# Three stages of a hybrid decoder step begin with another order of their seven products, and the entries of the feed-forward start are cast, split and summed in another order

## The chip, the cores and the metric

The kernel runs on one core of one Trainium2 chip. The metric is the device time of one launch in microseconds, the median of three runs. The core has a matrix engine (TensorE, PE in the profile), a vector engine (VectorE, DVE), an activation engine (ScalarE, ACT), a general engine (GpSimd, POOL) and a synchronising engine (SyncE, SP), which here only issues DMAs. Each engine executes its own queue in order and waits on semaphores of the others. Matmuls accumulate in banks of PSUM; DVE and ACT read those banks and write SBUF.

## The reference

One layer of a decoder on 512 prompt tokens and 8 sample tokens, with a model width of 2048 and a feed-forward width of 5632, in float32. What matters here, cut from the reference (the mixers' inside, the caches and the states are left out):

```python
def modulate(h, shift, scale):
    return h * (1.0 + scale) + shift

def conv_ffn(h, conv_state, w_ffn_in, conv_w, conv_b, w_ffn_out):
    T = h.shape[1]
    a, g = jnp.split(h @ w_ffn_in, 2, axis=-1)
    ap = jnp.concatenate([conv_state.astype(a.dtype), a], axis=1)
    ac = sum(conv_w[j] * ap[:, j:j + T] for j in range(CONV_W)) + conv_b
    out = (jax.nn.gelu(ac) * g) @ w_ffn_out
    return out, ap[:, ap.shape[1] - (CONV_W - 1):]
```

Ahead of this the normalised input is multiplied by `w_in`, which gives the mixers' inputs and the sigmoid gates of their outputs; the two mixers' outputs are projected, gated and added, and the sum is multiplied by `w_out` and added to the residual stream. The result, normalised and modulated, is the `h` of `conv_ffn`.

## The kernel before

The 520 tokens are two halves of 260 columns (`HN`), the 2048 channels 16 chunks of 128. For each multiplication of float32 precision both operands are split into a high part (a cast, on ACT, named `wh`, `hi` or the first half of `bf`, `mf`, `hf`) and a low part (the difference, on DVE, `wl`, `lo`), and each term is three matmuls: high by high, high by low, low by high (`three_of`).

The large stages multiply two blocks of weights by two halves of the channels and two halves of the tokens with seven products instead of eight. `Pair` (lines 256 to 338) is one such unit: seven products of 8 x 3 = 24 matmuls of 128 x 260, numbered 1 to 7. Products 1, 6, 7 and 4 accumulate one after another in the bank `x`, 5 and 3 in `y`, 2 in `z`. Product 1 takes the weights as they are, and so do 2 and 4; 5, 6, 3 and 7 take sums of weights, the totals 1, 2, 4 and 3 (`sw`), which `total` makes on DVE. `split` makes a product's `wh` and `wl`. Between two products of one bank `take` copies the bank to SBUF (`tt` after product 1 and after the first one in `y`, `tg` after 6) on ACT, and the next product into that bank waits for the copy; the combinations (`c12`, `c22`, `c11`) work on the copies. The order of the products in a unit is one of two tuples:

```python
ORDER, ORDER1 = (1, 5, 6, 3, 7, 2, 4), (1, 2, 3, 5, 6, 7, 4)
```

In `ORDER` the banks are x, y, x, y, x, z, x, in `ORDER1` x, z, y, y, x, x, x. The first unit of three stages has `ORDER1`, all others have `ORDER`. `run_pairs` goes through the products of all units, step by step, `7 * len(units)` of them: at step t it does what is due after the product before (`take`), prepares a product one or two steps ahead (`ahead`: splits and totals; `early` is 1 or 2), then any work listed for that step in the dictionary `late`, and at last issues the product. From `T, V, S = (Ordered(...))` on, the instructions of PE, DVE and ACT stay in the order in which they are written (line 60 is that helper, so they all carry L60); ahead of it a scheduler decides.

The three stages:

- The gates (from 554 us): `units` of `GatePair` and `ValuePair`. The first unit follows the projection of the stage before.
- w_out (from 1330 us): `units` of `WoPair`, which multiply the gated mixers' output `mg` (tiles `sgm`). In the loop over `w_pb` ahead of it each of 16 accumulations `pb` is multiplied by its gate and added to `mgo` (lines 1646, 1647). `m_first` and `m_forms` then make the seven forms of the tokens that the products use, from sums and differences of the chunks i and 8 + i; the forms 6 and 4 (`mf`) of the chunks below 7 are stored to DRAM (`dxf`) and loaded again later, so that their tiles are free meanwhile. The last chunk, 7, is made at the end of the loop.
- The feed-forward (from 1497 us). The first three feature chunks f are multiplied without the seven products, since their tokens' forms come one by one: `features(e, z)` makes the high and low parts of `h` for half e of the channels and half z of the tokens; `beside` and `eight(u, o, e, zs, w)` multiply an entry, which is the weight block (chunk u, o = 0 for the convolved and 1 for the gate side, half e) as it is, by them: 48 matmuls for both halves of the tokens. `sums_of(i)` turns the tokens of the chunks i and 8 + i into the sums that the seven products need, four operations on DVE each using the result of the one before; `sum_parts(n)` makes their high and low parts for product n. `parts2` makes an entry's `wh` and `wl`; `whole_conv(f)` and `whole_gate(f)` end a chunk (copy, convolution, Gelu, gate). Then come the units of `FfnPair`, from f = 3 on, the first of which begins at 1573.8 us.

Of the kernel before, what the change touches and what calls it, by code (L numbers as in the profile page):

```python
# [63 lines left out]
def tile_hybrid_step(ctx: ExitStack, tc: tile.TileContext, I, O):  # L64
# [189 lines left out]
    ORDER, ORDER1 = (1, 5, 6, 3, 7, 2, 4), (1, 2, 3, 5, 6, 7, 4)  # L254

    class Pair:
# [3 lines left out]
        def __init__(self, rows, X, order, early):  # L260
            self.rows, self.X, self.order, self.early = rows, X, order, early
            self.w, self.s = {}, {}
            self.uses = {(0, 0): 3, (1, 0): 2, (0, 1): 2, (1, 1): 2, 1: 2, 2: 2, 3: 1, 4: 1}
# [13 lines left out]
        def total(self, n):  # L277

            a, b = {1: ((1, 0), (1, 1)), 2: (1, (0, 0)), 4: ((0, 1), 2), 3: ((0, 0), (1, 0))}[n]
# [34 lines left out]
        def take(self, n):  # L314

            steady = self.order == ORDER
            if n == 1:
                self.tt = self.temp("tt")
                S.copy(self.tt[:, :HN], self.x)
            if n == (5 if steady else 3):  # L320
                S.copy(self.tt[:, HN:N], self.y)
            if n == 5 and not steady:
                V.tensor_tensor(self.tt[:, HN:N], self.y, self.tt[:, HN:N], op=ALU.subtract)
            if n == 6:
                self.tg = self.temp("tg")
                S.copy(self.tg[:, :HN], self.x)
            if n == (3 if steady else 6):
                self.c12()
            if n == 7:
                self.c22()  # L330
            if n == (2 if steady else 7):
                self.c11()
# [709 lines left out]
    class GatePair(Pair):  # L1042
        def __init__(self, gates, order):
            self.gates = gates
            super().__init__([I["w_in"][49 + g] for g in gates], hX, order, 1)
# [77 lines left out]
    units = [GatePair(gates[2 * i:2 * i + 2], ORDER if i else ORDER1) for i in range(len(gates) // 2)]  # L1123
# [361 lines left out]

    def m_forms(i):

        a, b = mg[i], mg[8 + i]
        mX[2][i], mX[3][i] = hl_parts(hp, "hl", b)
        b11, b12, b21, b22 = (t[:, o:o + HN] for t in (a, b) for o in (0, HN))  # L1490
        V.tensor_tensor(b11, b11, b12, op=ALU.subtract)
        V.tensor_tensor(b12, b22, b12, op=ALU.subtract)
        V.scalar_tensor_tensor(b22, b22, -1.0, b11, op0=ALU.mult, op1=ALU.subtract)
        V.scalar_tensor_tensor(b21, b22, -1.0, b21, op0=ALU.mult, op1=ALU.subtract)
        mX[5][i], mX[7][i] = hl_parts(hp, "hl", a)
        for n, f in ((6, b22), (4, b21)):
            t = (st if i == 7 else pt)("mf", F32R)
            hi, lo = mX[n][i] = parts_of(t)
            S.copy(hi, f)
            V.tensor_tensor(lo, f, hi.bitcast(F32), op=ALU.subtract)  # L1500
            if i < 7:
                G.dma_start(dxf[i + 8 * (n == 4)][:, :N], t[:, :N])
        mg[i] = mg[8 + i] = None
# [110 lines left out]
    for n, j in enumerate(order):  # L1614
# [31 lines left out]
        V.tensor_tensor(z2(mg[j]), acc, z2(mg[j]), op=ALU.mult)  # L1646
        V.tensor_tensor(mg[j][:, :N], mg[j][:, :N], old[:, :N], op=ALU.add)
        if j < 8:
            m_first(j)
        else:  # L1650
            m_forms(j - 8)
# [21 lines left out]
    def parts2(u, o, e):  # L1673
        return wtwo([raws.pop((u, o, e))], 1024)

# [33 lines left out]
    def first_weights(o):  # L1709
# [5 lines left out]
        9: log_exp, 50: lambda: fetch_xa(range(8)), 51: lambda: (load2(0, 0, 0), load2(0, 1, 0)), 53: tot_parts,  # L1715
# [79 lines left out]
    def whole_conv(f):  # L1795
        at = new_at()
        for z in range(2):
            S.copy(at[:, 2 + z * HN:2 + (z + 1) * HN], acc[f][0][z])
        acc[f][0] = None
        part[f] = conv_start(f, at)  # L1800
# [11 lines left out]
    def sums_of(i):  # L1812

        a, b = xa[i], xa[8 + i]
        b11, b12, b21, b22 = a[:, :HN], a[:, HN:N], b[:, :HN], b[:, HN:N]
        V.tensor_tensor(b11, b11, b12, op=ALU.subtract)
        V.scalar_tensor_tensor(b12, b22, dsh[:, i:i + 1], b12, op0=ALU.add, op1=ALU.subtract)
        V.scalar_tensor_tensor(b22, b22, shift(8 + i), b11, op0=ALU.add, op1=ALU.add)
        V.scalar_tensor_tensor(b21, b22, shift(8 + i), b21, op0=ALU.subtract, op1=ALU.subtract)
# [18 lines left out]
    features(0, 1, {0: lambda: W2.end(0), 2: lambda: W2.end(1), 3: lambda: half_squares(0), 6: lambda: ws.append(parts2(1, 0, 0))})  # L1838
# [11 lines left out]
    ws = some = None  # L1850
    w = parts2(1, 1, 0)
    load2(0, 1, 1)
    eight(1, 1, 0, (1, 0), w)
    some = [(0, 0, parts2(0, 0, 1))]
    load2(1, 0, 1)
# [4 lines left out]
    features(1, 1, {3: lambda: some.append((0, 1, parts2(0, 1, 1)))})  # L1860
    load2(2, 0, 0)
    beside(some, 1, 1)
    w = parts2(1, 0, 1)
    load2(2, 1, 0)
    features(1, 0)
# [5 lines left out]
    sums_of(0)  # L1871
    whole_conv(0)
    w0 = parts2(2, 0, 0)
    load2(1, 1, 1)
    eight(1, 0, 1, (0, 1), w)
    whole_gate(0)
    sums_of(1)
    acc.append([[t[:, z, :HN] for z in range(2)] for t in (acc_ps("fa"), acc_ps("fg"))])
    eight(2, 0, 0, (1, 0), w0)
    w0 = parts2(2, 1, 0)  # L1880
    load2(2, 0, 1)
    for i in range(2, 4):
        sums_of(i)
# [3 lines left out]
    w = parts2(1, 1, 1)  # L1887
    load2(2, 1, 1)
    for i in range(4, 6):
        sums_of(i)  # L1890
    whole_conv(1)
    eight(1, 1, 1, (0, 1), w)
    w0 = parts2(2, 0, 1)
    for i in range(6, 8):
        sums_of(i)
    eight(2, 0, 1, (0, 1), w0)
    w = parts2(2, 1, 1)
    sum_parts(5)
    whole_gate(1)
# [3 lines left out]
    class FfnPair(Pair):  # L1903
        def __init__(self, f, order):
            super().__init__((I["w_fi"][f], I["w_fi"][KF + f]), X, order, 2)
            self.f = f
# [238 lines left out]
    for k in range(KC):  # L2145
# [3 lines left out]
    units = [FfnPair(f, ORDER1 if f == 3 else ORDER) for f in range(3, KF)]  # L2149
# [3 lines left out]
    run_pairs(units, 2, {-2: lambda: eight(2, 1, 1, (0, 1), w), -1: lambda: (whole_conv(2), sum_parts(7)),  # L2153
                         0: lambda: whole_gate(2), 3: lambda: sum_parts(4),
# [104 lines left out]
```

## Time and profile before

| | |
|---|---|
| median of three runs | 2897.67 us (2895.3 to 2898.07) |
| the profiled execution, its time | 2895.6 us |
| its span in the profile | 2893.9 us |
| mean granted clock of TensorE | 0.998 |
| PE busy | 2847.5 us (98%) |
| DVE, ACT, POOL busy | 2156.6 us, 1367.1 us, 365.3 us |

A row of the timeline has the start in us from the span's start, the duration in us, the engine, the line, the operation, what it writes and reads without the buffers' numbers, the shape, the number of instructions that the row holds, and in brackets the idle time ahead of it on its engine with the instruction that ended it. A row of windows has the stretch, its length, the busy time of the engine with its instructions, the granted clock (1.00 is full), the DMA engines' share and their rate.

### The profile page before, as it was taken

What the parts mean: (1) busy time and instruction counts of PE and PEld (TensorE: products, weight loads), DVE (VectorE), ACT (ScalarE), POOL (GpSimd) and SP (SyncE); (2) the same over time, 40 slices, a digit from 0 to 9 for tenths busy, and PEclk for the clock granted to TensorE, in tenths of its full rate; (3) what the DMA queues carried; (4) which work ended last, traced back from release to release, by engine and by line L of the source; (5) the groups of instructions that cost most, each with busy time, mean ns of one, the idle gap of its engine ahead of it and who ended that gap; (6) DMA issues with size and microseconds to landing.
All of it is one profiled execution on the core that took longest, in us unless ns stands there. A gap on an engine that the chain in (4) does not pass through costs nothing. (4 is left out here: it accounts for less than half of the span.)

```text
span 2893.9 us, 58538 instructions
## 1 busy us (share of the span) xinstructions
PE 2847.5 (98%) x23460; PEld 2729.2 (94%) x23460; DVE 2156.6 (75%) x3994; ACT 1367.1 (47%) x2395; POOL 365.3 (13%) x649
## 2 busy tenths in 40 slices
PE   6999999999999999999999999999999999999999
PEld 4889998999998889899999999999999999999999
DVE  4776855577864566478889888888888887787787
ACT  3235643455544555334555444444444445544543
POOL 0001111211110122501211000000000001100100
PEclk9999999999999999999999999999999999999999
DMA  9933448844546576757763344444444436746742
GB/s 338 305 120 120 152 134 284 276 154 155 167 142 228 186 255 232 251 184 224 211 215 99 110 140 146 143 135 139 146 143 136 139 118 190 194 152 192 201 161 89
DMA packets 214137, 514.16 MB, mean 178 GB/s; under 512 B 24480, under 2 KB 77072, under 8 KB 213864
## 3 DMA queue, kind: packets, MB, share of 16 engines
q1 hardware_dynamic: 177072, 416.01, 44.5%
q0 software_dynamic: 36352, 94.18, 10.9%
q8 instruction: 184, 3.01, 0.4%
q14 instruction: 89, 0.73, 0.1%
q10 hardware_dynamic: 440, 0.23, 0.0%
HBM read 440.40 MB, written 66.46 MB: 175 GB/s over the span
## 5 line engine op out<-in xcount | busy, mean ns | idle before, releaser
L60 ACT CAST wh<-sw 128x512 fp32r<-128x512 f32 x640 | 366.8, 621 | 244.6 <-PE z L60 88.8
L60 PE MATMUL x<-bf,wh 128*128 128x260 f32 x2624 | 477.0, 283 | 1.0 <-DVE tg L60 0.5
L60 DVE TENSOR_TENSOR wl<-sw,wh 128x512 fp32r<-128x512 f32 x640 | 413.0, 688 | 83.5 <-ACT wh L60 80.6
L60 DVE TENSOR_TENSOR wl<-raw,wh 128x1024 fp32r<-128x1024 f32 (+2 forms) x325 | 338.0, 1052 | 119.6 <-ACT wh L60 112.6
L60 ACT CAST wh<-raw 128x1024 fp32r<-128x1024 f32 (+2 forms) x325 | 292.1, 912 | 266.7 <-PE x L60 129.8
L60 PEld LDWEIGHTS x<-bf,wh 128*128 128x128 f32 x2624 | 403.7, 188 | 1.4 <-DVE tg L60 0.7
L60 PE MATMUL x<-bf,wl 128*128 128x260 f32 x1312 | 370.2, 282 | 0.0
L178 DVE TENSOR_TENSOR wl<-raw,wh 128x1024 fp32r<-128x1024 f32 (+1 forms) x140 | 167.9, 1200 | 213.8 <-ACT wh L177 209.6
L177 ACT CAST wh<-raw 128x1024 fp32r<-128x1024 f32 (+1 forms) x140 | 144.0, 1029 | 236.7 <-issue 54.9
L60 PEld LDWEIGHTS x<-bf,wl 128*128 128x128 f32 x1312 | 246.7, 188 | 0.0
L60 PE MATMUL y<-bf,wh 128*128 128x260 f32 x1312 | 240.5, 284 | 2.9 <-ACT wh L60 2.4
L60 PEld LDWEIGHTS y<-bf,wh 128*128 128x128 f32 x1312 | 202.9, 189 | 3.3 <-ACT wh L60 2.6
L60 DVE TENSOR_TENSOR sw<-raw,raw 128x512 f32<-128x512 f32 x316 | 203.5, 686 | 0.7 <-DMA tot<-sq 0.6
L60 PE MATMUL x<-ff,wh 128*128 128x260 f32 x1024 | 186.2, 283 | 0.0
L60 PE MATMUL y<-bf,wl 128*128 128x260 f32 x656 | 185.7, 283 | 0.2 <-DVE wl L60 0.2
L60 PEld LDWEIGHTS x<-ff,wh 128*128 128x128 f32 x1024 | 157.5, 188 | 0.0
L60 PE MATMUL x<-ff,wl 128*128 128x260 f32 x512 | 144.4, 282 | 0.0
L60 PE MATMUL x<-hf,wh 128*128 128x260 f32 x720 | 130.7, 282 | 1.0 <-ACT wh L60 0.6
L60 PE MATMUL fo<-fe,wh 128*128 128x260 f32 x768 | 125.9, 284 | 1.6 <-DVE fo L60 1.1
L60 PEld LDWEIGHTS y<-bf,wl 128*128 128x128 f32 x656 | 124.3, 190 | 0.4 <-DVE wl L60 0.4
L60 PE MATMUL z<-bf,wh 128*128 128x260 f32 x656 | 121.5, 286 | 0.0
L60 PEld LDWEIGHTS z<-bf,wh 128*128 128x128 f32 x656 | 100.9, 189 | 13.4 <-issue 13.4
(603 smaller groups left out, 7564.1 us busy)
## 6 DMA issues: line engine op xcount, KB each, us to landing
raw<-in_w_fi SPq DMA_DIRECT2D x176, 512.0 KB, 4.1
raw<-in_w_in SPq DMA_DIRECT2D x156, 512.0 KB, 4.7
ar<-in_w_ada SPq DMA_DIRECT2D x192, 256.0 KB, 6.1
raw<-in_w_ada SPq DMA_DIRECT2D x96, 512.0 KB, 4.2
raw<-in_w_fo SPq DMA_DIRECT2D x64, 512.0 KB, 3.9
raw<-in_w_out SPq DMA_DIRECT2D x32, 512.0 KB, 4.7
raw<-in_w_fo SPq DMA_DIRECT2D x32, 384.0 KB, 3.8
dff<-cc POOLq DMA_DIRECT2D x44, 260.0 KB, 3.6
```

What stands on the lines that cost most here:

```text
L60: return lambda *a, **k: self.tc.keep_in_program_order(getattr(self.eng, op)(*a, **k))
L177: S.copy(wh[:, o], t[:, :m])
L178: V.tensor_tensor(wl[:, o], t[:, :m], wh[:, o].bitcast(F32), op=ALU.subtract)
```

## The change

`ORDER1` becomes (1, 3, 6, 5, 7, 2, 4), banks x, y, x, y, x, z, x; only w_out's first unit has it still. The first units of the gates and of the feed-forward have `ORDER` like the rest. In w_out the forms of the last chunk are made in pieces (`m_second`, `m_sums`, `m_parts`) as late entries of the steps 0, 1 and 4, and total 4 and the split of product 3 are made ahead of the loop's end. In the feed-forward an entry's cast (`cast2`) and its low part (`low2`) are issued apart, some of them between the steps of `features`; the entries (1, 0, 1) and (1, 1, 1) of the second chunk are multiplied ahead of the third chunk's, with (1, 1, 1) drawn forward; `sums_of` takes two chunks and alternates their operations; and the parts for the products 6, 7 and 4, the third chunk's convolution and its gate move to other steps of the first unit.

The diff, cut:

```diff
-    ORDER, ORDER1 = (1, 5, 6, 3, 7, 2, 4), (1, 2, 3, 5, 6, 7, 4)
+    ORDER, ORDER1 = (1, 5, 6, 3, 7, 2, 4), (1, 3, 6, 5, 7, 2, 4)
...
-                for n in ({-1: (1,), 0: (2,), 1: (4,), 2: (3,)} if self.order == ORDER else
-                          {-1: (1, 2), 0: (4,), 2: (3,)}).get(r, ()):
+                for n in {-1: (1,), 0: (2,), 1: (4,), 2: (3,)}.get(r, ()):
...
-    units = [GatePair(gates[2 * i:2 * i + 2], ORDER if i else ORDER1) for i in range(len(gates) // 2)]
+    units = [GatePair(gates[2 * i:2 * i + 2]) for i in range(len(gates) // 2)]
...
+    def m_second(i):
+        mX[2][i], mX[3][i] = hl_parts(hp, "hl", mg[8 + i])
...
+    def m_parts(i, n):
+        if n == 5:
+            mX[5][i], mX[7][i] = hl_parts(hp, "hl", mg[i])
+            return
+        f = quarters(i)[3 if n == 6 else 2]
+        t = (st if i == 7 else pt)("mf", F32R)
+        hi, lo = mX[n][i] = parts_of(t)
+        S.copy(hi, f)
+        V.tensor_tensor(lo, f, hi.bitcast(F32), op=ALU.subtract)
...
                 units[0].total(2)
+                units[0].total(4)
                 turn[0] = 2
-                units[0].split(2)
+                units[0].split(3)
...
+        elif j < KC - 1:
+            m_forms(j - 8)
         else:
-            m_forms(j - 8)
+            m_second(7)
...
+    def cast2(u, o, e):
+        turn[0] += 1
+        wh, wl = ((cf if turn[0] % 3 == 0 else wp).tile([P, 1024], F32R, tag=t, name=nm(t)) for t in ("wh", "wl"))
+        raw = raws.pop((u, o, e))
+        S.copy(wh, raw)
+        return wh, wl, raw
+
+    def low2(w):
+        wh, wl, raw = w
+        V.tensor_tensor(wl, raw, wh.bitcast(F32), op=ALU.subtract)
+        return wh, wl
...
     run_pairs(units, 2, {
-        9: log_exp, 50: lambda: fetch_xa(range(8)), 51: lambda: (load2(0, 0, 0), load2(0, 1, 0)), 53: tot_parts,
+        0: lambda: (m_sums(7, 0), m_sums(7, 1), m_parts(7, 6)), 1: lambda: (m_parts(7, 5), m_sums(7, 2)),
+        4: lambda: (m_parts(7, 4), mg.clear()), 9: log_exp, 50: lambda: fetch_xa(range(8)), 51: lambda: (load2(0, 0, 0), load2(0, 1, 0)), 53: tot_parts,
...
+    features(1, 1, {1: lambda: (cast(1, 1, 0), load2(0, 1, 1)), 3: lambda: low(ws),
+                    4: lambda: (cast(0, 0, 1), load2(1, 0, 1)), 6: pair_low,
+                    7: lambda: (cast(0, 1, 1), load2(1, 1, 1)), 9: pair_low})
+    eight(1, 1, 0, (1, 0), ws.pop())
     beside(some, 1, 1)
-    w = parts2(1, 0, 1)
-    load2(2, 1, 0)
-    features(1, 0)
+    features(1, 0, {1: lambda: (cast(1, 0, 1), load2(2, 0, 0)), 4: lambda: low(ws)})
...
+    eight(1, 1, 1, (0, 1), w)
+    cast(2, 0, 0)
+    load2(2, 0, 1)
+    sums_of(4, 5)
+    w0 = low2(casts.pop())
     eight(2, 0, 0, (1, 0), w0)
...
-    units = [FfnPair(f, ORDER1 if f == 3 else ORDER) for f in range(3, KF)]
+    units = [FfnPair(f) for f in range(3, KF)]
...
-    run_pairs(units, 2, {-2: lambda: eight(2, 1, 1, (0, 1), w), -1: lambda: (whole_conv(2), sum_parts(7)),
-                         0: lambda: whole_gate(2), 3: lambda: sum_parts(4),
+    run_pairs(units, 2, {-2: lambda: eight(2, 1, 1, (0, 1), w), -1: lambda: whole_copy(2),
+                         1: lambda: sum_parts(7), 2: lambda: whole_conv(2), 3: lambda: sum_parts(4),
+                         4: lambda: whole_gate(2),
```

ACT at the start of w_out, before: `mf` are forms of the last chunks, `wh` weights' high parts, `tt` the copy of bank `x` after product 1 and of `y`.

```order
L1476 CAST mf_16189<-sgm_15012 128x520
L1476 CAST mf_16197<-sgm_15751 128x520
L1499 CAST mf_16201<-sgm_15012 128x260
L1499 CAST mf_16204<-sgm_15012 128x260
L60 CAST wh_16240<-sw_16236 128x512
L60 CAST wh_16240<-sw_16238 128x512
L60 COPY tt_16277<-x_16250 128x260
L60 CAST wh_16283<-sw_16175 128x512
L60 CAST wh_16283<-sw_16177 128x512
```

The copy `tt<-x` stood behind total 4's casts there. The same place after the change:

```order
L1478 CAST mf_16194<-sgm_15011 128x520
L60 CAST wh_16227<-sw_16178 128x512
L60 CAST wh_16227<-sw_16180 128x512
L60 CAST mf_16240<-sgm_15011 128x260
L60 COPY tt_16270<-x_16243 128x260
L60 CAST wh_16276<-sw_16174 128x512
L60 CAST wh_16276<-sw_16176 128x512
L60 CAST mf_16284<-sgm_15750 128x520
L60 COPY tt_16270<-y_16244 128x260
```

The copy stands now directly behind one `mf<-sgm` of 260 columns, the high part of the last chunk's form for product 6, and the casts for total 2 (product 6's weights) stand ahead of that form.

DVE at the same place, before, from the last `pb` but one:

```order
L1646 TENSOR_TENSOR sgm_15751<-pb_16054,sgm_15751 128x520
L1647 TENSOR_TENSOR sgm_15751<-sgm_15751,mgo_16052 128x520
L1484 TENSOR_TENSOR mf_16109<-sgm_15751,mf_16109 128x260
L1491 TENSOR_TENSOR sgm_15751<-sgm_15751 128x260
L1646 TENSOR_TENSOR sgm_15012<-pb_16118,sgm_15012 128x520
L1647 TENSOR_TENSOR sgm_15012<-sgm_15012,mgo_16116 128x520
L1492 TENSOR_TENSOR sgm_15751<-sgm_15012,sgm_15751 128x260
L1477 TENSOR_TENSOR mf_16190<-sgm_15012,mf_16189 128x520
L1477 TENSOR_TENSOR mf_16198<-sgm_15751,mf_16197 128x520
L1493 SCALAR_TENSOR_TENSOR sgm_15012<-sgm_15012,sgm_15751 128x260
L1494 SCALAR_TENSOR_TENSOR sgm_15012<-sgm_15012 128x260
L1500 TENSOR_TENSOR mf_16201<-sgm_15012,mf_16201 128x260
```

And after the change:

```order
L1668 TENSOR_TENSOR sgm_15750<-pb_16053,sgm_15750 128x520
L178 TENSOR_TENSOR wl_16187<-sw_16182,wh_16186 128x512
L178 TENSOR_TENSOR wl_16187<-sw_16184,wh_16186 128x512
L1669 TENSOR_TENSOR sgm_15750<-sgm_15750,mgo_16051 128x520
L1668 TENSOR_TENSOR sgm_15011<-pb_16117,sgm_15011 128x520
L1486 TENSOR_TENSOR mf_16108<-sgm_15750,mf_16108 128x260
L1669 TENSOR_TENSOR sgm_15011<-sgm_15011,mgo_16115 128x520
L1479 TENSOR_TENSOR mf_16195<-sgm_15011,mf_16194 128x520
L60 TENSOR_TENSOR wl_16228<-sw_16178,wh_16227 128x512
L60 TENSOR_TENSOR wl_16228<-sw_16180,wh_16227 128x512
L60 TENSOR_TENSOR sgm_15750<-sgm_15750 128x260
L60 TENSOR_TENSOR sgm_15750<-sgm_15011,sgm_15750 128x260
```

Behind the last `pb` but one stand now the low parts of the weights of product 3 (`wl_16187`), and between the last `pb` and the last chunk's sums (`sgm<-sgm`, and the SCALAR_TENSOR_TENSOR) those of product 6 (`wl_16228`).

DVE at the first unit of the feed-forward, before: `cc` is the third chunk's convolution, `bf` low parts of the token sums, `sw` totals of weights, `wl` low parts of weights.

```order
L60 SCALAR_TENSOR_TENSOR cc_19367<-at_19363,sv,cc_19367 128x512 x2
L60 SCALAR_TENSOR_TENSOR cc_19367<-stc,sv,cc_19367 128x8 x2
L60 TENSOR_TENSOR bf_19376<-xa_18175,bf_19376 128x260
L60 TENSOR_TENSOR bf_19378<-xa_18177,bf_19378 128x260
L60 TENSOR_TENSOR bf_19381<-xa_18179,bf_19381 128x260
L60 TENSOR_TENSOR bf_19384<-xa_18181,bf_19384 128x260
L60 TENSOR_TENSOR bf_19387<-xa_18183,bf_19387 128x260
L60 TENSOR_TENSOR bf_19390<-xa_18185,bf_19390 128x260
L60 TENSOR_TENSOR bf_19393<-xa_18187,bf_19393 128x260
L60 TENSOR_TENSOR bf_19396<-xa_18189,bf_19396 128x260
L60 TENSOR_TENSOR sw_19400<-raw_19297,sw_19355 128x512
L60 TENSOR_TENSOR sw_19402<-raw_19297,sw_19357 128x512
```

Here eight low parts of one form stand between the convolution and total 4 (`sw_19400`). After the change:

```order
L60 TENSOR_TENSOR sw_19354<-sw_19298,raw_19290 128x512
L60 TENSOR_TENSOR sw_19356<-sw_19300,raw_19290 128x512
L60 TENSOR_TENSOR wl_19359<-sw_19298,wh_19358 128x512
L60 TENSOR_TENSOR wl_19359<-sw_19300,wh_19358 128x512
L60 TENSOR_TENSOR sw_19368<-raw_19296,sw_19354 128x512
L60 TENSOR_TENSOR sw_19370<-raw_19296,sw_19356 128x512
L60 TENSOR_TENSOR wl_19373<-sw_19354,wh_19372 128x512
L60 TENSOR_TENSOR wl_19373<-sw_19356,wh_19372 128x512
L60 TENSOR_TENSOR sw_19407<-raw_19290,raw_19292 128x512
L60 TENSOR_TENSOR sw_19409<-raw_19290,raw_19292 128x512
L60 TENSOR_TENSOR wl_19412<-sw_19368,wh_19411 128x512
L60 TENSOR_TENSOR wl_19412<-sw_19370,wh_19411 128x512
```

The totals and the low parts of their weights follow one another, and the convolution and the eight low parts come behind these rows.

More of the change, by code (lines that the diff above doesn't have):

```diff
@@ L1042, in tile_hybrid_step, with __init__ @@
     class GatePair(Pair):
-        def __init__(self, gates, order):
+        def __init__(self, gates):
             self.gates = gates
-            super().__init__([I["w_in"][49 + g] for g in gates], hX, order, 1)
+            super().__init__([I["w_in"][49 + g] for g in gates], hX, ORDER, 1)
         def temp(self, name):
@@ L1793, in tile_hybrid_step, with whole_copy @@
     part = {}
-    def whole_conv(f):
-        at = new_at()
+    def whole_copy(f):
+        part[f] = at = new_at()
         for z in range(2):
@@ L1799, in whole_conv @@
         acc[f][0] = None
+    def whole_conv(f):
+        if f not in part:
+            whole_copy(f)
+        at = part[f]
         part[f] = conv_start(f, at)
@@ L1836, in sum_parts, with cast, low @@
                     V.tensor_tensor(lo, src[j - 1], hi.bitcast(F32), op=ALU.subtract)
-    features(0, 1, {0: lambda: W2.end(0), 2: lambda: W2.end(1), 3: lambda: half_squares(0), 6: lambda: ws.append(parts2(1, 0, 0))})
+    casts, some = [], []
+    def cast(*x):
+        casts.append(cast2(*x))
+    def low(out):
+        out.append(low2(casts.pop()))
+    features(0, 1, {0: lambda: W2.end(0), 2: lambda: W2.end(1), 3: lambda: half_squares(0),
+                    4: lambda: cast(1, 0, 0), 6: lambda: low(ws)})
     load2(0, 0, 1)
@@ L1870, in tile_hybrid_step @@
     r2 = None
-    sums_of(0)
+    sums_of(0, 1)
+    cast(1, 1, 1)
+    load2(2, 1, 0)
+    sums_of(2, 3)
+    eight(1, 0, 1, (0, 1), w)
+    w = low2(casts.pop())
     whole_conv(0)
-    w0 = parts2(2, 0, 0)
-    load2(1, 1, 1)
-    eight(1, 0, 1, (0, 1), w)
     whole_gate(0)
-    sums_of(1)
     acc.append([[t[:, z, :HN] for z in range(2)] for t in (acc_ps("fa"), acc_ps("fg"))])
-    eight(2, 0, 0, (1, 0), w0)
[L1880 to L1883, printed above, removed]
+    eight(1, 1, 1, (0, 1), w)
[3 more added lines that the diff above has]
+    w0 = low2(casts.pop())
+    eight(2, 0, 0, (1, 0), w0)
+    whole_conv(1)
+    cast(2, 1, 0)
+    load2(2, 1, 1)
+    sums_of(6, 7)
+    w0 = low2(casts.pop())
     eight(2, 1, 0, (1, 0), w0)
@@ L1886, in tile_hybrid_step @@
         hb.pop((i, 1))
[L1887 to L1895, printed above, removed]
+    sum_parts(5)
+    cast(2, 0, 1)
+    whole_gate(1)
+    w0 = low2(casts.pop())
     eight(2, 0, 1, (0, 1), w0)
     w = parts2(2, 1, 1)
-    sum_parts(5)
-    whole_gate(1)
     sum_parts(6)
```

77 lines of the change are left out of this document (42 added, 35 removed).

## The prediction

> **What bounds the kernel now.** I read the page first: one engine carries the span.
>
> ```profile
> PE 2847.5 (98%) x23460; PEld 2729.2 (94%) x23460; DVE 2156.6 (75%) x3994; ACT 1367.1 (47%) x2395; POOL 365.3 (13%) x649
> ```
>
> TensorE is busy 98%, so a reordering that leaves the number of matmuls alone can only win the places where PE stands still or runs slowly. The windows over the three starts that the change touches (gates; w_out; features; first FFN pair) say how much is there: stretch, length, busy time, matmuls, granted clock.
>
> ```profile
> 553.00:578.00 25.00, 23.50 (x192) 1.00 0.91 283
> 1328.00:1356.00 28.00, 24.82 (x198) 1.00 0.84 267
> 1493.00:1545.00 52.00, 48.94 (x376) 0.97 0.37 122
> 1545.00:1602.00 57.00, 52.93 (x420) 0.97 0.30 97
> ```
>
> The timeline of PE names each wait; the bracket is the idle time and its releaser. Gates first, then w_out:
>
> ```profile
> 563.63 0.51 PE L60 MATMUL y<-hf,wh 128*128 128x260 f32 x2 [0.47 <-ACT tt L60]
> ...
> 570.08 0.51 PE L60 MATMUL x<-hf,wh 128*128 128x260 f32 x2 [0.47 <-ACT tg L60]
> ...
> 573.76 0.48 PE L60 MATMUL x<-hf,wh 128*128 128x260 f32 x2 [0.57 <-ACT wh L60]
> ...
> 1337.41 0.51 PE L60 MATMUL y<-mf,wh 128*128 128x260 f32 x2 [1.23 <-ACT wh L60]
> 1338.14 0.39 PE L60 MATMUL y<-mf,wl 128*128 128x260 f32 x1 [0.22 <-DVE wl L60]
> ...
> 1341.52 0.51 PE L60 MATMUL y<-mf,wh 128*128 128x260 f32 x2 [0.47 <-ACT tt L60]
> ...
> 1348.03 0.50 PE L60 MATMUL x<-mf,wh 128*128 128x260 f32 x2 [0.46 <-ACT tg L60]
> ...
> 1351.96 0.51 PE L60 MATMUL x<-mf,wh 128*128 128x260 f32 x2 [0.80 <-DVE tg L60]
> ```
>
> Then one wait in the features, and the first FFN pair with the undisturbed rows ahead of it:
>
> ```profile
> 1532.96 0.92 PE L60 MATMUL fa<-bf,wh 128*128 128x260 f32 x2 [0.86 <-ACT bf L60]
> ...
> 1579.16 0.40 PE L60 MATMUL z<-bf,wh 128*128 128x260 f32 x2
> 1579.40 0.28 PE L60 MATMUL z<-bf,wl 128*128 128x260 f32 x1
> 1582.08 0.51 PE L60 MATMUL y<-bf,wh 128*128 128x260 f32 x2 [2.40 <-ACT wh L60]
> 1582.81 0.39 PE L60 MATMUL y<-bf,wl 128*128 128x260 f32 x1 [0.22 <-DVE wl L60]
> ...
> 1584.13 0.64 PE L60 MATMUL y<-bf,wh 128*128 128x260 f32 x2
> ...
> 1584.78 0.64 PE L60 MATMUL y<-bf,wh 128*128 128x260 f32 x2
> ...
> 1587.70 0.51 PE L60 MATMUL y<-bf,wh 128*128 128x260 f32 x2 [0.47 <-ACT tt L60]
> ...
> 1594.16 0.50 PE L60 MATMUL x<-bf,wh 128*128 128x260 f32 x2 [0.47 <-ACT tg L60]
> ...
> 1597.83 0.51 PE L60 MATMUL x<-bf,wh 128*128 128x260 f32 x2 [0.52 <-DVE tg L60]
> ```
>
> Two matmuls start 0.24 us apart from 1579.16 to 1579.40: 0.12 us each, undisturbed. By that the windows lost 25 − 192 × 0.12 = 2.0 us at the gates, 28 − 198 × 0.12 = 4.2 at w_out, 52 − 376 × 0.12 = 6.9 in the features, 57 − 420 × 0.12 = 6.6 at the FFN start. The brackets give less (1.51, 3.18, 4.08 at gates, w_out, FFN), for the matmul behind a wait is drawn out too (0.51 for 0.40). And after the 2.40 us PE ran slowly: three matmuls from 1584.13 to 1584.78 take 0.65 us instead of 0.36. At that pace the about 3.4 us from 1583.3 to 1586.7 lose 3.4 × (1 − 0.36/0.65) = 1.5 us. That is inside the 6.6.
>
> **The change, part by part.**
>
> *Gates.* In the first pair, one product ends in the bank in which the next begins at three places, and PE waits for the copy (tt, tg) that empties it; with the order 1, 5, 6, 3, 7, 2, 4 no two neighbours share a bank, and each copy has a whole product (24 × 0.12 = 2.9 us) to be done in. This is the order of every later pair, which runs without those waits. The third wait, for a weight cast, stood behind the tg copy on ACT and goes as well. Nothing is added. Gain 2.0.
>
> *w_out.* The old five waits go, 4.2 us. But the new order 1, 3, 6, 5, 7, 2, 4 needs the form for product 6 third, where it was fifth, and DVE makes its weights before it. These are rows of DVE's and ACT's timelines in order of time:
>
> ```profile
> 1328.17 0.69 DVE L1646 TENSOR_TENSOR sgm<-pb,sgm 128x520 f32<-128x520 f32 x1
> ...
> 1332.35 1.16 ACT L1476 CAST mf<-sgm 128x520 fp32r<-128x520 f32 x2 [2.30 <-DVE sgm L1647]
> 1333.01 1.31 DVE L1477 TENSOR_TENSOR mf<-sgm,mf 128x520 fp32r<-128x520 f32 x2 [0.23 <-ACT mf L1476]
> 1334.23 0.42 DVE L1493 SCALAR_TENSOR_TENSOR sgm<-sgm,sgm 128x260 f32<-128x260 f32 x1
> 1334.69 0.88 ACT L1499 CAST mf<-sgm 128x260 fp32r<-128x260 f32 x2 [1.19 <-DVE sgm L1493]
> 1335.94 1.29 DVE L60 TENSOR_TENSOR sw<-raw,sw 128x512 f32<-128x512 f32 x2
> 1337.39 1.30 DVE L60 TENSOR_TENSOR wl<-sw,wh 128x512 fp32r<-128x512 f32 x2 [0.16 <-ACT wh L60]
> 1337.79 0.37 ACT L60 COPY tt<-x 128x260 f32<-128x260 f32 x1
> ```
>
> The chain on DVE, from the old time of the first sgm<-pb: total 4 is now added before it, 1.2 (the pair of sw rows takes 1.29, its successors overlapping it a little), to 1329.4; sgm<-pb of j = 14 0.6, two wl for product 3 1.25, product by mgo 0.6, sgm<-pb of j = 15 0.6, one low part 0.35, product by mgo 0.7 (the additions and products are of one shape), to 1333.5. ACT casts the 520 columns, half of 1.16, and DVE makes its low part, half of 1.31: 1334.9. Two wl for product 6, 1.25: 1336.1. Three sums at 0.45 (the row at 1334.23 and its like): 1337.4. ACT casts the form, half of 0.88, and only then, queued behind that cast, makes the copy tt<-x, 0.37, which product 6 needs to write x: 1338.2, and PE sees it 0.1 later. PE is through products 1 and 3 at 1336.1, when the old row too was waiting (1337.41 less 1.23 is 1336.2). So one wait of about 2.2 us stands where there were five. Later forms (5, 7 and 4) have a product or more each; I charge them nothing, with 0.5 as the price if one is late. Net gain 4.2 − 2.2 = 2.0.
>
> A second cost can stand ahead of this. Total 4's tile is freed by a store of a form:
>
> ```profile
> dxf<-mf POOLq DMA_DIRECT2D x6, 260.0 KB, 3.9
> ```
>
> Issued about 1325, at the median it lands at 1328.9, and DVE has nothing to wait for. A landing 1 us later passes through DVE to sgm<-pb, which PE needs to reuse the bank: 0 to 1 us; I take 0.
>
> *Features.* Cast and low part of an entry are apart, and the cast of the next weights is made between two bf. The wait at 1532.96 arose because DVE made wl (1.2) and three xa ahead of the bf that ACT waited for; split, the cast comes a few steps earlier. I take 0.86 and the drawn-out neighbours, 1.3 in all, as gained; between 0 and 1.5. The larger losses, up to 1504, come ahead of the first moved instruction and stay.
>
> *Sums two chunks at a time.* Four dependent operations of a chunk become eight, alternating, so none waits for the one before it. DVE is not the bound there, so it counts only through lateness. The tightest place is the second chunk's first entry, now ahead of (2, 0, 0). Its low part stands on DVE behind the first chunk's Gelu gate (rows of before, where an entry's cast and low part stand between):
>
> ```profile
> 1540.59 1.03 ACT L60 CAST wh<-raw 128x1024 fp32r<-128x1024 f32 x1
> ...
> 1542.66 1.21 DVE L60 TENSOR_TENSOR wl<-raw,wh 128x1024 fp32r<-128x1024 f32 x1
> ...
> 1542.82 1.28 ACT L60 ACT_TABLE_LOAD   x1 [1.19 <-DVE cc L60]
> ...
> 1544.78 0.76 DVE L60 TENSOR_TENSOR cc<-fg,cc 128x260 f32<-128x260 f32 x2 [0.91 <-ACT cc L60]
> ```
>
> Ending at 1545.5 less the 1.3 us of the previous item, 1544.2, then two chunks' sums (8 of the like of the 0.42 at 1334.23, each start 0.35 to 0.4 after the last: about 3.0) and wl 1.2: 1548.4 at the latest; with the convolution starting a little sooner, 1547.5. PE wants it after three more entries of 48 × 0.12 = 5.8 us, near 1548. Wait 0 to 0.5 us, I take 0.3.
>
> *First FFN pair.* Before, the wait of 2.40 came from total 4, third of DVE's tasks behind low parts:
>
> ```profile
> 1577.92 2.80 DVE L60 TENSOR_TENSOR bf<-xa,bf 128x260 fp32r<-128x260 f32 x8
> 1580.64 1.29 DVE L60 TENSOR_TENSOR sw<-raw,sw 128x512 f32<-128x512 f32 x2
> ```
>
> Now product 5 comes second, which needs total 1, made first of all; total 4 stands ahead of the last eight low parts, and its product, 3, is fourth. The low parts for 7 (2.80) move to step 1 and the convolution to step 2, each with nearly 3 us of product before its reader. All five waits go, and the slow stretch with the wait: 6.6, less 0.4 for a late cast of the last product's weights, which is now behind 16 bf. Gain 6.2.
>
> [...]
>
> **Sum.** −2.0 −2.0 −1.3 +0.3 −6.2 = −11.2. On the profiled 2895.6 us that makes 2884.4; the median of the runs shown lies 2.1 higher, 2897.67, and 11.2 off it is 2886.5. I round to 2886.7.
>
> **The rivals.**
> - *The one w_out wait slows the clock, or the store is late.* 2.2 us is near 2.40, which did it; the 1.23 us at 1337.41 did not (that window's clock is 1.00). If it does, 1.5 us more, and up to 1 for the store: gain 11.0 − 2.5 = 8.5, 2889.2. Chance 0.27.
> - *DVE falls behind in the features.* If low parts for (2, 0, 0), (2, 1, 0) and (2, 0, 1) each come 1 us late and one such wait slows the clock, 4.5 go: 2891.2; if the first pair's 2.4 returns too, with its slow stretch, 2895. Against it: DVE has about 3 us less to do. Chance 0.13.
> - *Slow stretch of another origin.* If it is not the 2.40 that causes it, it stays, 1.5: 2888.2. Chance 0.05. [...]
> - *Slower.* The split casts take a weight pair from a rotation (each third from another pool) earlier than before. If ACT's in-order queue then stands at a cast whose pair PE still reads, the bf behind it are late, and each entry starts only after cast and low part, 1.05 + 1.2 us, late: six entries, 13.5 us, and the gain becomes a loss of 2.5; with half the clock behind three of them, 4.5 more, a loss of 7: 2904.7. It decides from the point where a cast has to wait for the entry just ahead of it; three pairs in rotation speak against it. Chance 0.06.
> - *Nothing measurable:* starts gained are spent again in the next pair's weights. Chance 0.04; 2897.
>
> **How the numbers follow.** The forecast has 0.45. A measurement of this kernel can tell about 0.2%, 5.8 us. The forecast, the w_out rival and the other origin are faster, 0.77, and of the DVE case half, 0.06: 0.83. The other half and "nothing" make 0.1 the same; 0.07 slower. The range begins at 2883.7 (no new wait at w_out beyond 1 us, nothing at the entries, and the whole features term) and ends at 2894.0, most of the way into the DVE case.
>
> **What would show it.** After: no tt or tg wait on PE in the three first pairs; one wait of about 2.2 us at the third w_out product, released by ACT's tt; none of 2.4 behind wh at the FFN start and a clock of 1.00 there; nothing of 0.86 in the features. Wrong would be: a clock under 1.00 behind the w_out wait, waits on wl at fa<-bf or fg<-bf between 1540 and 1575, or ACT idle behind PE at a cast of the entries.

## The result, and the profile after

The changed kernel takes 2881.84 us, the median of six runs (2880.41 to 2889.95), beside 2894.55 us for the kernel before in six runs (2893.55 to 2898.07): a ratio of 0.9959 with a 95% interval of 0.9948 to 0.9969. It is faster by about 12.7 us of medians. The forecast said faster by 11.0, at 2886.7, in a range whose low end is 2883.7, so the time lies 1.9 us below it. The profiled execution took 2881.72 us, with a span of 2880.0 instead of 2893.9.

The same four windows after the change, shifted by what was gained before each (stretch, length, PE busy time with matmuls, clock, DMA share, GB/s):

```profile
551.00:576.00 25.00, 25.00 (x211) 1.00 1.01 299
1324.00:1352.00 28.00, 26.17 (x217) 1.00 0.87 271
1488.00:1540.00 52.00, 49.15 (x392) 1.00 0.40 130
1540.00:1592.00 52.00, 51.12 (x423) 1.00 0.31 97
```

The gates are full. PE's timeline has one wait left at w_out, and these in the feed-forward's start (the first three of the features, as before, are left out):

```profile
1335.55 0.51 PE L60 MATMUL x<-mf,wh 128*128 128x260 f32 x2 [1.83 <-ACT tt L60]
...
1500.67 0.39 PE L60 MATMUL fa<-bf,wh 128*128 128x260 f32 x1 [0.59 <-DVE bf L60]
...
1521.00 0.39 PE L60 MATMUL fg<-bf,wl 128*128 128x260 f32 x1 [0.22 <-DVE wl L60]
...
1544.49 0.39 PE L60 MATMUL fa<-bf,wl 128*128 128x260 f32 x1 [0.62 <-DVE wl L60]
...
1585.27 0.47 PE L60 MATMUL x<-bf,wh 128*128 128x260 f32 x2 [0.20 <-DVE tg L60]
```

None of the old tt and tg waits is there, nor the 2.40 us; a tg wait of 0.20 us at the last product of the feed-forward's first unit is new. The 1.83 us at w_out is the one forecast wait; ACT's timeline shows the copy queued behind the cast of the last form, as the chain had it:

```profile
1334.81 0.41 ACT L60 CAST mf<-sgm 128x260 fp32r<-128x260 f32 x1 [2.19 <-DVE sgm L60]
1335.13 0.37 ACT L60 COPY tt<-x 128x260 f32<-128x260 f32 x1
```

To compare kernels, I add up by how much the starts of successive matmuls lie further apart than 0.12 us ("lost" below; it holds waits, matmuls drawn out behind them and slow clock alike). The stretches are: 24 us from the first gates product, 26 us from the first w_out product, from 4 us ahead of the first feature product to 30 behind it, the next 17 us, from there to the first unit, 31 us of the first unit.

| lost, us | gates | w_out | features | around the 0.86 wait | entries | first unit |
|---|---|---|---|---|---|---|
| before | 2.27 | 4.51 | 4.93 | 1.58 | 0.00 | 6.94 |
| after | 0.00 | 2.29 | 4.70 | 0.00 | 1.21 | 0.44 |
| gain | 2.3 | 2.2 | 0.2 | 1.6 | −1.2 | 6.5 |

That is 11.6 us. (Counted with the few longer matmuls of the norm, `ms`, the features come to 5.30 and 5.00, nearly the same difference.) The other 2.3 of the 13.9 us between the spans lie in stretches that the edit leaves alone. By the starts of the stages' first products, 0.95 of them lie between gates and w_out (in before PE waits 1.0 us there for a low part, in after it does not), 0.6 between w_out and the features, 0.15 from there to the first unit and 1.3 behind its start, of which 0.8 are in the feed-forward's later units, told below; less 0.7, by which after came to the gates later. Why they differ was not tried.

### The profile page after: what moved, and what is told of

Same layout as the page of the kernel before. It is cut to its first block, busy times and chain, and to the rows that moved or that the text cites. A ratio compares the mean times of both kernels' runs of the same rounds, so it can differ in the third digit from the quotient of the medians.

```text
span 2880.0 us, 58532 instructions
## 1 busy us (share of the span) xinstructions
PE 2840.4 (99%) x23460; PEld 2723.7 (95%) x23460; DVE 2151.4 (75%) x3992; ACT 1366.4 (47%) x2395; POOL 361.3 (13%) x649
## 5 line engine op out<-in xcount | busy, mean ns | idle before, releaser
L60 PEld LDWEIGHTS z<-bf,wh 128*128 128x128 f32 x656 | 100.4, 188 | 13.4 <-issue 13.4
```

The lines of the kernel that those rows point to most:

```text
L60: return lambda *a, **k: self.tc.keep_in_program_order(getattr(self.eng, op)(*a, **k))
```

## The experiments

The runs were taken in four sessions: that of the result, and three later ones. In each, before was run again beside the others, and a kernel's time is compared with before's of the same session.

**The gates alone** (`gates_only`). `made` only keeps a total from being made twice.

```diff
-    units = [GatePair(gates[2 * i:2 * i + 2], ORDER if i else ORDER1) for i in range(len(gates) // 2)]
+    units = [GatePair(gates[2 * i:2 * i + 2]) for i in range(len(gates) // 2)]
```

> Before with the new order at the gates' first unit alone. Theory (each bank wait is worth its own time and nothing is handed back): the three waits of 0.47, 0.47 and 0.57 us are gone, 2.0 to 2.3 us less than before, w_out and the feed-forward keep their waits. Rival (later waits on DMAs or on the next unit's weights take it back): waits gone, but the time within 0.5 us of before. Second rival (where the clock's slow stretches fall depends on the time at which the idle falls): the slow stretches behind 1501 and 1583 us come or go with a shift of 2 us, 1.5 us each, so 0.5 to 5 us less.

2901.32 us beside 2901.65, ratio 0.9996 (0.9987 to 1.0005). The first stretch lost 0.00 instead of 2.27, as the theory has it, but in this execution w_out lost 6.82 and the features 6.00: at w_out the last wait of the first unit was 1.79 us instead of 0.80, and 3.41 us at half clock followed it.

```profile
1356.44 0.69 PE L60 MATMUL x<-mf,wh 128*128 128x260 f32 x2 [1.79 <-DVE tg L60]
...
1589.83 0.50 PE L60 MATMUL y<-bf,wh 128*128 128x260 f32 x2 [2.40 <-ACT wh L60]
```

The edit changes no instruction there. DVE was late for that wait because it had stood still for a load; the row of before and that of this run:

```profile
1348.47 0.48 DVE L60 SCALAR_TENSOR_TENSOR x<-tg,ada,x 128x252 f32<-128x252 f32 x1
```
```profile
1352.94 0.48 DVE L60 SCALAR_TENSOR_TENSOR x<-tg,ada,x 128x252 f32<-128x252 f32 x1 [1.04 <-DMA x<-in_xT]
```

In `old_wout`, the other kernel with the gates' new order and the old w_out, DVE waits 0.60 us for the same load and the last wait is 1.35 us; in `ffn_only` and `ffn_order`, with the old gates, it does not wait. So the first rival has it in the time (0.3 us less) and has a load to point to, which gives back 1.0 of the 2.3 us in this execution; whether it does so in every execution, two traces do not show. Behind the 2.40 us the clock stayed full this time (1.00 from 1585.28 to 1595.52; first unit 5.40 lost, not 6.94), so the second rival holds too: a gain of 2 us cannot be told in the time from the clock's and the session's scatter. The theory's 2.0 to 2.3 us show in the stretch itself, not in the time.

**The feed-forward alone** (`ffn_only`), all parts of the diff from the features on.

> Before with the changes from the features on alone; gates and w_out as before. Theory: the wait of 0.86 us in the features, the 2.40 us and the three small ones of the first unit are gone, a wait of 0.6 us on a low part appears at the third chunk's first entry; 5.5 to 6.5 us less than before. Rival (the rearranged casts and sums bring less than the order): under 4 us. The slow stretch at the start of the features is outside of what is changed: if it stays, the change cannot have taken it away; if it is gone, it goes by chance of phase.

2896.01 us, 5.6 less than before's 2901.65, ratio 0.9977 (0.9968 to 0.9987). Lost: around the 0.86 wait 0.00, entries 1.16, first unit 0.45; so 1.58 − 1.16 + 6.49 = 6.9 by the trace of before, of which 1.5 are its slow stretch. The theory is right. The slow stretch of the features is missing here (4.73), in `gates_only` it is there (6.00), and neither edit changes an instruction of the first features.

**After with the old w_out** (`old_wout`).

> After with w_out as it was (order 1, 2, 3, 5, 6, 7, 4 there, forms made at once). Theory: the five old waits come back, 4.5 us lost at w_out in place of the one wait's 2.0 to 2.3: 2.2 us more than after. Rival (the new order gains nothing net, the gain of after at w_out is execution noise): within 0.5 us of after.

2893.15 us, ratio 0.9964 (0.9951 to 0.9977). w_out lost 5.06: the five waits are back, the last one 1.35 us instead of 0.80 (the load told above). The new w_out's 2.29 is 2.2 to 2.8 less. The trace shows it; the time, taken without after beside it, does not by itself.

**The cast behind the copy** (`copy_first`).

```diff
-        0: lambda: (m_sums(7, 0), m_sums(7, 1), m_parts(7, 6)), 1: lambda: (m_parts(7, 5), m_sums(7, 2)),
+        0: lambda: (m_sums(7, 0), m_sums(7, 1)), 1: lambda: (m_parts(7, 6), m_parts(7, 5), m_sums(7, 2)),
```

> After with the high part of the last chunk's form for product 6 made one step later, behind the copy of bank x instead of ahead of it. Theory (the one w_out wait is the copy queued on ACT behind that cast, which waits for DVE; the last chunk of the form is read only by the last three matmuls of the product): the wait of 1.83 us is gone or under 0.3, 1.7 to 2.0 us less than after. Rival (DVE is the chain itself, weights and sums are late whatever the queue): a wait of 1 us or more stays, at the first or the last matmuls of product 6, at most 1 us less.

2889.17 us, ratio 0.9952 (0.994 to 0.9965). The copy no longer waits and product 6 starts at once, but the wait moved to its end:

```profile
1349.26 0.39 PE L60 MATMUL x<-mf,wh 128*128 128x260 f32 x1 [1.22 <-DVE mf L60]
```

DVE's timeline says why: the form's low part had come behind the sums and low parts of the next weights.

```profile
1346.37 1.29 DVE L60 TENSOR_TENSOR sw<-raw,raw 128x512 f32<-128x512 f32 x2
1347.58 1.29 DVE L60 TENSOR_TENSOR wl<-sw,wh 128x512 fp32r<-128x512 f32 x2
1348.78 1.03 DVE L60 TENSOR_TENSOR mf<-sgm,mf 128x260 fp32r<-128x260 f32 x2
```

Lost at w_out: 1.69 for 2.29, so the rival's wait of over 1 us at the last matmuls is what came. The theory named the right queue and the rival the next one: I had moved an instruction that stands between two queues and followed only one. The time, taken without after beside it, does not decide.

**After once more** (`after_again`), in another session.

> After, unchanged, beside the others on one chip. Theory (the edit's own gain is the sum of its local waits, about 11 us, and the rest of the 13.9 us between the two profiled spans is clock phase and a pace that differs between executions): 10 to 12.5 us less than before. Rival (the whole 13.9 is the edit's): 13.5 to 14.5 us less. At the features' start the idle time stays the same 1.1, 0.2 and 0.6 us whether or not a slow stretch follows.

2881.54 us beside 2894.78, ratio 0.995 (0.9936 to 0.9964), 13.2 us less: above the theory's 12.5 and under the rival's 13.5. The waits at the features' start are 1.14, 0.21 and 0.62 us, as expected. The same wait of w_out is there, and this time the clock dropped behind it. Windows of 3.41 us around it, of this execution and of the earlier one of after (how they were laid is told in the last section):

```profile
1332.50:1335.91 3.41, 1.59 (x14) 1.00 1.23 391
1335.91:1339.33 3.42, 3.42 (x19) 0.50 0.74 234
1339.33:1342.74 3.41, 3.41 (x30) 1.00 0.41 153
```
```profile
1330.68:1334.09 3.41, 3.04 (x26) 1.00 1.23 394
1334.09:1337.50 3.41, 1.95 (x16) 1.00 1.11 356
1337.50:1340.92 3.42, 3.42 (x31) 1.00 0.78 260
```

So w_out lost 3.78 us here and 2.29 there by the same instructions and the same wait (1.82 us, from 1333.24 to 1335.06, and 1.83 us, from 1333.72 to 1335.55).

**Two moves** (`both`): the form's high and low part behind the copy, and two entries' low parts ahead of the sums.

```diff
+    def take_form(n):
+        take0(n)
+        if n == 1:
+            m_parts(7, 6)
...
+    w0 = low2(casts.pop())
     sums_of(4, 5)
-    w0 = low2(casts.pop())
...
+    w0 = low2(casts.pop())
     sums_of(6, 7)
-    w0 = low2(casts.pop())
```

> After with two moves: the last chunk's form for product 6 (high and low part) made directly behind the copy of bank x and ahead of the next weights on DVE, and the low parts of the entries (2, 0, 0) and (2, 1, 0) made ahead of the sums of two chunks instead of behind them. Theory: no wait of over 0.3 us at w_out's product 6 (1.83 before, 1.22 at the product's end when only the cast was moved), none at the third chunk's first two entries (0.62); 2.5 to 3 us less than after. Rival (the DVE work is only passed on): a wait of 0.5 to 1.5 us at product 5 of w_out or at the entry (2, 0, 1), and less than 1.5 us gained.

2879.87 us, 1.7 less than after beside it (ratio to before 0.9947, 0.9934 to 0.9961); w_out lost 1.14, the entries 0.25 instead of 1.20. The 1.82 and 0.60 us are gone, as the theory has it; 0.48 appears at product 5, close to the rival's 0.5, where the copy of bank y stood behind another cast:

```profile
1339.61 0.50 PE L60 MATMUL y<-mf,wh 128*128 128x260 f32 x2 [0.48 <-ACT tt L60]
```

The 1.7 us lie between the theory's 2.5 and the rival's 1.5, and the intervals of the two ratios to before overlap.

**The order alone in the first feed-forward unit** (`ffn_order`).

```diff
-    units = [FfnPair(f, ORDER1 if f == 3 else ORDER) for f in range(3, KF)]
+    units = [FfnPair(f, ORDER) for f in range(3, KF)]
```

> Before with the new order of products in the feed-forward's first unit alone, casts, sums and steps as they were. Theory (the 2.40 us came from total 4 behind eight low parts, needed third in the old order and fourth in the new one): the 2.40 wait falls below 0.5 us and the tt and tg waits go, 3.5 to 5 us less than before. Rival (the queue on DVE is what is late, and the moves of the parts for product 7 and of the convolution are needed): a wait of 1 us or more on a weight stays at the second to fourth product; 1 to 3 us less than before.

2892.93 us, ratio 0.9991 (0.9982 to 1.0). First unit 3.18 lost instead of 6.94 (5.40 where the clock stayed full): the order is worth 2.2 to 3.8 us, the rest needs the other moves. The rival has it:

```profile
1582.73 0.50 PE L60 MATMUL x<-bf,wh 128*128 128x260 f32 x2 [0.85 <-ACT tt L60]
...
1584.58 0.39 PE L60 MATMUL x<-bf,wl 128*128 128x260 f32 x1 [1.35 <-DVE wl L60]
```

On DVE the eight low parts for product 7 (2.80 us from 1579.93) still stand ahead of product 6's low parts, and on ACT the copy of x stands behind the third chunk's Gelu.

**The sums one chunk after the other** (`one_sum`). The one loop of four operations in place of four loops of one.

> After with the two chunks' sums one chunk after the other again (the calls at the same places). Theory (alternating them saves the waits between dependent operations, 0.35 us a chunk, 0.7 us a pair): the wait at the entry (2, 0, 0) grows from 0.62 to about 1.3 us and a second one of about 0.5 to 1 appears at (2, 1, 0), 1 to 1.5 us more than after. Rival (DVE has slack there): no change beyond 0.3 us at these entries.

2886.47 us, 4.9 more than after beside it, ratio 0.9968 (0.9955 to 0.998). The two chunks' sums take 3.82 us, from 1541.17 to 1544.99, against 3.08 in after (1540.14 to 1543.22), as expected; the wait is far longer than expected, because the two earlier pairs of sums had pushed the chain back too (it starts 1.0 us later, in an execution whose features began 0.5 us earlier):

```profile
1541.17 0.42 DVE L60 TENSOR_TENSOR xa<-xa 128x260 f32<-128x260 f32 x1
...
1544.99 1.22 DVE L60 TENSOR_TENSOR wl<-raw,wh 128x1024 fp32r<-128x1024 f32 x1
```
```profile
1540.14 0.76 DVE L60 TENSOR_TENSOR xa<-xa 128x260 f32<-128x260 f32 x2
...
1543.22 1.22 DVE L60 TENSOR_TENSOR wl<-raw,wh 128x1024 fp32r<-128x1024 f32 x1
```
```profile
1546.26 0.58 PE L60 MATMUL fa<-bf,wl 128*128 128x260 f32 x1 [2.85 <-DVE wl L60]
```

The granted clock was 0.50 from 1545.36 to 1552.19; 5.75 us were lost at the entries instead of 1.2. The alternating sums are what keeps the change from this.

**Three moves** (`three_moves`) **and after a third time** (`after_third`), beside each other. The third move, as a cut of the diff against the version with two:

```diff
+        if n == 3:
+            m_parts(7, 5)
...
-        1: lambda: (m_parts(7, 5), m_sums(7, 2)),
+        1: lambda: m_sums(7, 2),
```

> The kernel with the two moves (form for product 6 behind the copy of bank x, low parts of two entries ahead of the sums) and a third one: the high and low parts of the last chunk's form for product 5 behind the copy of bank y instead of ahead of it on ACT. Theory (the 0.48 us left at product 5 is that copy queued behind this 520-column cast): no wait over 0.25 us at w_out's first unit; about 2.5 us less than after in waits (1.83 and 0.62 gone), up to 4 where after's own wait slows the clock. Rival (the cast made later is late itself): the 0.48 us comes back at the last matmuls of product 5 or at the tg copy, and no gain over the two moves. By the placement of the token forms (as in after) the feed-forward units' pace is 620.47 us from the first to the last adaLN group of that stage.

> After, unchanged, beside the version with three moves. Its waits are those of the other two executions (1.8 us at w_out, 0.6 at the entry (2, 0, 0)); a slow stretch of about 3.3 us follows the 1.8 us or not, by chance. Theory: 12 to 14 us less than before, and 2 to 4 more than the version with three moves; rival: the three moves bring under 1 us.

2887.56 us beside 2890.43 for after and 2903.81 for before (ratios 0.9949, 0.9936 to 0.9962, and 0.9954, 0.9942 to 0.9967). So the version with three moves is 2.9 us faster than after by medians, five of its six runs below the fastest of after's five, though the intervals of the two ratios overlap. That is what `after_third` expected: 13.4 us less than before, 2.9 more than the three moves, w_out's wait 1.82 us, this time with no slow clock behind it (pairs of matmuls from 1347.93 on take 0.40 us, behind the same wait in `after_again` 0.64). The third move missed its own theory: the copy's 0.48 us turned into 0.45 of the same product's `wl`, over the 0.25 allowed, and w_out lost 1.16, no more gained than by two moves (whose ratio to before, 0.9947, is the same within the intervals). It brought nothing that shows.

## Why the prediction was wrong, and where it was right

- **Gates, 2.0:** right; 2.27 lost before, 0.00 after. That 2 us cannot be seen in the time is part of the answer.
- **w_out, 2.0 net:** right with its mechanism. One wait, 1.83 us for 2.2, at product 6, released by ACT's tt behind the form's cast. Of the 0.4 us too much, 0.16 is a slip of the sum (from 1333.5, half of 1.16 and half of 1.31 give 1334.7 and not 1334.9), 0.17 is PE, which came through products 1 and 3 at 6.02 us from its first w_out product where the prediction has 5.85, and 0.05 is PE's start behind the copy, 0.05 us after its end (1335.13 + 0.37 to 1335.55) where the prediction has 0.1. The store's landing did no harm: total 4 starts at 1325.66 with no wait.
- **Rival of the clock at w_out (0.27):** it came in one of three profiled executions of after (w_out lost 2.29, 3.78, 2.27). The prediction asked whether 2.2 us is long enough; the length did not decide it, as the clock was 0.50 behind 1.82 us and 1.00 behind 1.83 us (last section).
- **Features, 1.3:** 1.58, right. That the larger losses up to 1504 stay was right for the waits (1.14, 0.20, 0.61 again), wrong for the slow stretch behind them: it is there in before (clock 0.50 from 1501.36 to 1504.77) and absent in after's first profile (1.00 from 1488 to 1540). With it absent, PE ran on to a new wait of 0.59 at 1500.67, so that gave only 0.2.
- **Entries, −0.3:** too small; 0.62 us of wait, 1.2 lost with the matmuls around it and 0.3 at the next entry. The place and the cause (the low part behind gate and sums) were right, and moving the low part ahead takes it away. Of the three late low parts of the DVE rival that is one, and no slow clock followed it here (1.00 from 1540 to 1592).
- **First unit, 6.2:** 6.5; of it 1.5 hang on a slow stretch that the same kernel part need not have (`gates_only` kept the 2.40 us without it).
- **The sum, 11.2, came out at 11.6** in the stretches changed. That it is so close is partly luck: the entries cost 0.9 us more than forecast, and the other four terms gained 0.2 to 0.5 more each.
- **The step that failed is the level** from which the gain was taken. "The median of the runs shown lies 2.1 higher, 2897.67" took three runs for the level, while before's level was 2894.55 with six, 2894.78, 2901.65 and 2903.81 in later sessions. Of the 4.9 us by which the time lies under the forecast, 3.1 are this level, 1.5 the gain (12.7 by medians for 11.2), and 0.2 the rounding. The range was built of the edit's terms alone, with nothing for the level: its low end, 2883.7, allowed 14.0 us from 2897.67, which from 2894.55 would have been 2880.6 and held the time. The 14.0 is itself more than its words add up to: 2.0 + 3.2 (4.2 less a wait of 1.0) + 1.5 + 6.6 = 13.3 at the most.
- **A second omission:** I took every stretch outside the edit to be unchanged, a term of nothing. Between the two profiles it was 2.3 us; 0.8 of them is the feed-forward's own pace (last section), and the rest is placed but not explained.

Where the session's level comes from shows in the traces of the sessions with the higher level. In a stretch of the gate projections that no edit touches, PE waits for nothing that the profile shows, 7.1 us in twelve pieces in `copy_first`, none in after; its clock there is low too:

```profile
PE gate L223 <- issue: 7.1, 12, 1.1
```
```profile
1161.00:1168.00 7.00, 4.63 (x22) 0.78 0.88 309
1168.00:1176.00 8.00, 5.55 (x27) 0.56 0.42 130
```
```profile
1161.00:1168.00 7.00, 7.00 (x61) 1.00 0.89 293
1168.00:1176.00 8.00, 6.75 (x56) 1.00 0.80 263
```

The first two fences are of `copy_first`, the last of after. All six traces of the two sessions with the higher level have such pauses, 3.9 to 7.1 us, and none of the six of the other two sessions. From the first gates product to the first w_out product after took 772.64 us and `after_third` 784.47, which is 11.8 of the 12.3 us between their spans. What holds PE there was not tried.

## What to carry to other kernels

Two products in a row that share an accumulation bank cost a wait for the copy between them here (0.47 us); the order that alternates banks has none of it in the gates (2.27 us lost before, 0.00 after), but it also changes which operand is needed early, and the in-order queue that makes this operand then has to be read instruction by instruction on every engine, low part and copy included. Moving one instruction out of a queue's way can leave its partner on another engine in the way: in `copy_first` the cast went first, and in place of the 1.83 us came a wait of 1.22 us for its low part. For changes of a few tenths of a per cent, forecast the difference against before in the same session, and give the level a spread of its own.

## What the runs showed of the hardware

**Half clock followed a wait of 1.82 us in one execution and not one of 1.83 us in another, of one kernel.** The granted clock behind them was 0.50 in `after_again` and 1.00 in after; behind the 2.40 us it was 0.50 in before and 1.00 in `gates_only`. The expectations put this down to chance. In the trace of before the clock changes at 33.63, 40.45, 1501.36, 1504.77, 1583.28 and 1586.69, in that of after at 33.61 and 40.43, each in us from the span's start, and in either trace these times lie whole multiples of 3.413 us apart (in before, half clock begins at 1501.36 and at 1583.28, 24 x 3.413 us later). The slow stretch lasts 3.41 us behind the 2.40 us of before and behind the waits at w_out in `after_again` and `gates_only`, and 6.83 us behind the 2.85 us of `one_sum`. The windows shown for the run `after_again` have edges at such multiples: where half clock followed, the whole wait lies in one window; in the other execution the edge at 1334.09 (379 x 3.413 us behind its change of clock at 40.43) cuts it in two, 0.37 and 1.46 us. The same of the 2.40 us, in before and in `gates_only`, where the edge at 1588.69 cuts it:

```profile
1579.87:1583.28 3.41, 0.98 (x6) 1.00 0.10 16
1583.28:1586.69 3.41, 3.41 (x18) 0.50 0.68 220
```
```profile
1585.28:1588.69 3.41, 2.15 (x18) 1.00 0.00 0
1588.69:1592.11 3.42, 2.06 (x15) 1.00 0.36 95
1592.11:1595.52 3.41, 2.94 (x25) 1.00 0.70 213
```

Of the eight single waits of 1.79 to 2.85 us in the first unit of w_out, at the third chunk and in the first unit of the feed-forward, half clock followed four: the 2.40 us of before, the 1.82 of `after_again`, the 1.79 of `gates_only` and the 2.85 of `one_sum`, which left PE busy for 0.98, 1.59, 1.62 and 1.46 us of one window. Behind the other four the clock stayed full; in the two of them shown here PE was busy for 1.95 us (after) and 2.06 us (`gates_only`) or more of every window. This gives no threshold: in before, windows busy for 1.86 us (1497.95 to 1501.36) and, at half clock, 2.03 us (33.63 to 37.04) were followed by half clock, where the 1.95 us of after were followed by full clock. The windows were laid over the traces afterwards, and no run moved a wait against such edges on purpose: that the place of the wait decides is not shown.

**The same instructions run at four paces, which differ by up to 0.2% and repeat to 0.01 us.** In the later feed-forward units the same instructions run in all these kernels. The rows of the adaLN groups of that stage, of before and after (count, ns least/median/most, first and last start in us):

```profile
L60 PE MATMUL adp<-ar,cs x128: 592/605/617, 1675.6 to 2297.3; 128*32 128x512 f32 x128
```
```profile
L60 PE MATMUL adp<-ar,cs x128: 592/605/617, 1662.9 to 2283.9; 128*32 128x512 f32 x128
```

That is 621.7 and 621.0 us. From the start of the first group to that of the last, the five kernels with the new w_out and feed-forward have 620.46 or 620.47 us in seven executions, `ffn_only` and `old_wout` both 621.60, before and `gates_only` both 621.23, `ffn_order` 620.87. In the programs built from these kernels the weights and banks of the 5040 matmuls between these groups lie at the same addresses in all, and the token forms differ from set to set in 720 to 1800 of them, within a set in 90 at most; the edits ahead of that stage decide this through the tile pools. Product by product the link holds only in part. Product 6, whose forms lie at the same place in all, takes 2.875 us on average in all; product 2 takes 2.93 us in the kernels with the old place of its forms and 2.915 in after and `copy_first`, where half of them lie elsewhere. But product 5, whose forms also lie at the same place in all, takes 2.878 us in before, 2.880 in `old_wout`, 2.871 in `ffn_order` and 2.866 in after. Placement was not changed by itself, so the link is observed, and what sets the pace stays open.
